# A softmax streamed through one buffer: four loads become two, and two late loads become one

## The chip, the cores and the metric

The kernel runs on one core of a Trainium2 chip. The metric is device time in microseconds (us) of one execution. Every profile is of one further execution, with times in us from the start of its span.

## The reference

```python
x = np.random.randn(16, 1024, 512).astype(np.float32)
x_scaled = x / 2.0
exp_x = np.exp(x_scaled - np.max(x_scaled, axis=-1, keepdims=True))
out = exp_x / np.sum(exp_x, axis=-1, keepdims=True)
```

This is a softmax over 512 elements for each of 16,384 rows, at temperature 2. Input and output have 33.55 MB each, and nothing is read twice, so 67.1 MB have to pass the DMA engines.

## The kernel before, in words

**Tiles.** The 16,384 rows are 128 per partition. In this text "a row" is one such row on all 128 partitions: 512 floats on each, 2 KB a partition, 256 KB in all. `TILES` cuts the 128 rows into ten tiles, numbered 0 to 9: 3, 5, and then eight times 15 rows, each with its place in the buffer. The buffer, `arena`, holds 98 rows. Tiles 0 to 7 fill it; tile 8 comes to rows 0 to 14 and tile 9 to rows 15 to 29, over what tiles 0 to 3 held. A tile of r rows is read from a contiguous block of memory so that partition p gets one contiguous run of r rows; a 15-row tile is 128 runs of 30,720 bytes. The output has the same layout.

**Loads** (`load`, L114). SP (the queue called q1 in the profile) issues the load of tile 0, and ACT (q10) at once the loads of tiles 1 to 7, one DMA each, before it computes anything. GpSimd (POOL, q0) issues the two late loads. It first waits until the exponentials of all rows ahead of row 83 are done (`TURN`, L178: tiles 0 to 6), then, for each late tile, until the stores that free its place have landed: `LATE` says stores 0, 1, 2 for tile 8 and store 3 for tile 9 (L179 to L181). Each load has its semaphore `ld`. TensorE does nothing but pass these on (L196): when load t has landed, it raises `s_go` by the number of chunks in tile t.

**Exponentials** (`exponentials`, L275 in the profile; L206 for the first three rows). ACT takes one unit of `s_go` per chunk of 5 rows, and for each row writes exp(x/2) over the row in place and its sum into `stats`. There is no maximum; the data need none, and a fallback at the end redoes everything if a sum is out of range. It does not run here.

**Division** (L168, L171). DVE takes the reciprocals of the sums of one tile (of 5 rows for the last tile), and multiplies the tile in place.

**Stores** (`store`, L135 to L139). SP issues them in the order of the tiles, each after its multiplication. `SPREAD = 1` makes the store of tile 1 three DMAs: four rows of it as 128 runs of 8,192 bytes, then the fifth row as 126 runs of 2,048 bytes, then the same row's last 2 runs. Before store 2, SP waits until stores 0 and 1 have landed in all their pieces (L214, L215; the profile shows this as a wait of L137 for a DMA). The stores behind it in SP's program wait with it. At the end SP waits for the last landings (L261).

Each transfer of 128 runs is spread over the core's 16 DMA engines, 8 runs on each, and every engine finishes its share with one 4-byte write to the semaphore, here called its marker. In the profile each run and each marker is one packet. A 15-row tile has 128 + 16 = 144 packets.

Of the kernel before, what the change touches and what calls it, by code (L numbers as in the profile page):

```python
# [10 lines left out]
    (3, 0), (5, 3), (15, 8), (15, 23), (15, 38), (15, 53), (15, 68), (15, 83), (15, 0), (15, 15),  # L11
]

LATE = {8: (0, 1, 2), 9: (3,)}
ARENA = 98

HEAD = [3]
# [2 lines left out]
SPREAD = 1  # L20
# [8 lines left out]
def kernel(  # L29
# [5 lines left out]
    nc = tc.nc  # L35
# [6 lines left out]
    xf = x.flatten_outer_dims()  # L42
    of = out.flatten_outer_dims()
    N, D = xf.shape
    P = nc.NUM_PARTITIONS
# [14 lines left out]
    tiles, base = [], 0  # L60
# [2 lines left out]
        tiles.append((base, r, at))  # L63
        base += r

    def dram(ap, t):
        b, r, _ = tiles[t]
        return ap[b * P : (b + r) * P].rearrange("(p r) d -> p r d", r=r)

    def sb(t):  # L70
        _, r, at = tiles[t]
        return arena[:, at : at + r, :]

    straight = sum(HEAD)
# [3 lines left out]
    owner = [max(t for t, (b, _, _) in enumerate(tiles) if b <= s) for s in starts]  # L78
# [9 lines left out]
            pairs.append([k])  # L88
    upto = [1 + max(j for j, ks in enumerate(pairs) if owner[ks[0]] == t) for t in range(len(tiles))]

    ld = [nc.alloc_semaphore(f"ld{t}") for t in range(len(tiles))]
    s_home = {t: nc.alloc_semaphore(f"s_home{t}") for t in LATE}
    s_near = nc.alloc_semaphore("s_near")
    s_end = nc.alloc_semaphore("s_end")
    s_exp = nc.alloc_semaphore("s_exp")
    s_go = nc.alloc_semaphore("s_go")
    s_rec = nc.alloc_semaphore("s_rec")
    s_mul = nc.alloc_semaphore("s_mul")
# [11 lines left out]
    g_rec = nc.alloc_semaphore("g_rec")  # L110
    g_mul = nc.alloc_semaphore("g_mul")

    def load(eng, t):
        eng.dma_start(out=sb(t), in_=dram(xf, t)).then_inc(ld[t], 16)  # L114

    def pieces(t):
        r = tiles[t][1]
        if t == SPREAD:
            return [(0, P, 0, r - 1), (0, 126, r - 1, r), (126, P, r - 1, r)]
        return [(0, P, 0, r)]  # L120

    stored_by = {u: s_home[t] for t, us in LATE.items() for u in us}
    for t, (_, r, at) in enumerate(tiles):
        over = {u for u, (_, ru, au) in enumerate(tiles[:t]) if at < au + ru and au < at + r}
        assert over <= {u for v, us in LATE.items() if v <= t for u in us}

    def landings(ts):
        return 16 * sum(len(pieces(t)) for t in ts)

    near = len(tiles) - 2  # L130
    sem_of = {**stored_by, near: s_near}
    at_end = landings(t for t in range(len(tiles)) if t not in sem_of)

    def store(eng, t):
        eng.wait_ge(s_mul, upto[t])  # L135
        for p, q, lo, hi in pieces(t):
            eng.dma_start(  # L137
                out=dram(of, t)[p:q, lo:hi], in_=sb(t)[p:q, lo:hi]
            ).then_inc(sem_of.get(t, s_end), 16)  # L139

    def take(eng, sem, n):
        eng.wait_ge(sem, n).then_inc(sem, -n)  # L142

    def rounds(eng, body):


        i = eng.alloc_register("general")
        eng.wait_ge(s_near, 16)
        eng.wait_ge(s_flag, 1)
        eng.reg_load(i, flag[0:1, 0:1])  # L150
        with eng.While(lambda: eng.snap(i, min_val=0, max_val=1) < 1):
            body()
            eng.reg_add(i, i, 1)

    def early():
        load(nc.sync, 0)
        load(nc.scalar, 1)

    def loads():
        for t in range(2, min(LATE)):  # L160
            load(nc.scalar, t)

    def program():

        for j, ks in enumerate(pairs):
            b, c = starts[ks[0]], sum(sizes[k] for k in ks)
            a = b % ARENA
            nc.vector.reciprocal(  # L168
                out=recip[:, b : b + c], in_=stats[:, b : b + c]
            )._wait_ge(s_exp, ks[-1] + 1).then_inc(s_rec, 1)  # L170
            nc.vector.tensor_mul(  # L171
                out=arena[:, a : a + c],
                in0=arena[:, a : a + c],
                in1=recip[:, b : b + c].unsqueeze(2).to_broadcast([P, c, D]),
            )._wait_ge(s_rec, j + 1).then_inc(s_mul, 1)

        nc.gpsimd.memset(ones[:, :], 1.0).then_inc(s_ones, 1)  # L177
        nc.gpsimd.wait_ge(s_exp, starts.index(TURN))  # L178
        for t, us in LATE.items():  # L179
            nc.gpsimd.wait_ge(s_home[t], landings(us))  # L180
            load(nc.gpsimd, t)  # L181
        nc.gpsimd.tensor_scalar(  # L182
            out=inside[:, :], in0=stats[:, :], scalar1=LO, scalar2=HI,
            op0=Alu.max, op1=Alu.min,
        )._wait_ge(s_exp, len(sizes)).then_inc(s_cnt, 1)
        nc.vector.scalar_tensor_tensor(  # L186
            out=inside[:, :], in0=inside[:, :], scalar=1.0, in1=stats[:, :],
            op0=Alu.mult, op1=Alu.is_equal, accum_out=count[:, :],
        )._wait_ge(s_cnt, 1).then_inc(s_cnt, 1)
        nc.vector.tensor_scalar(  # L190
            out=flag[:, :], in0=total[:, :], scalar1=float(N), scalar2=None, op0=Alu.is_ge,
        )._wait_ge(s_tot, 1).then_inc(s_flag, 1)


        for t in range(len(tiles)):
            nc.tensor.wait_ge(ld[t], 16).then_inc(s_go, owner.count(t))  # L196
        nc.tensor.wait_ge(s_ones, 1)
        nc.tensor.matmul(  # L198
            total[:, :], lhsT=count[:, :], rhs=ones[:, :], start=True, stop=True
        )._wait_ge(s_cnt, 2).then_inc(s_tot, 1)  # L200

        nc.scalar.preload_act_table(Exp)  # L202
        for k, c in enumerate(HEAD):
            take(nc.scalar, s_go, 1)
            for b in range(starts[k], starts[k] + c):
                ins = nc.scalar.activation(  # L206
                    out=arena[:, b], in_=arena[:, b], func=Exp, scale=0.5,
                    accum_out=stats[:, b : b + 1],
                )
            ins.then_inc(s_exp, 1)  # L210
        exponentials(straight, n_rows)

        for t in range(len(tiles)):
            if t == SPREAD + 1:  # L214
                nc.sync.wait_ge(s_home[min(LATE)], landings(range(t)))  # L215
            store(nc.sync, t)

        x_g = xf.rearrange("(t p r) d -> t p r d", p=P, r=G)  # L220
        o_g = of.rearrange("(t p r) d -> t p r d", p=P, r=G)
        data = arena[:, 0:G]

        def vector():
            for i in range(n_rows // G):
                nc.vector.reduce_max(
                    out=g_max[:, :], in_=data, axis=mybir.AxisListType.X, negate=True
                )._wait_ge(g_go, i + 1).then_inc(g_top, 1)
                nc.vector.reduce_sum(
                    out=g_sum[:, :], in_=data, axis=mybir.AxisListType.X  # L230
                )._wait_ge(g_exp, i + 1).then_inc(g_add, 1)
                nc.vector.reciprocal(
                    out=g_sum[:, :], in_=g_sum[:, :]
                )._wait_ge(g_add, i + 1).then_inc(g_rec, 1)

        def scalar():
            for i in range(n_rows // G):
                nc.scalar.activation(out=data, in_=data, func=Exp, scale=0.5)._wait_ge(
                    g_sub, i + 1
                ).then_inc(g_exp, 1)  # L240

        def gpsimd():
            nc.gpsimd.wait_ge(s_end, at_end)
            for i in range(n_rows // G):
                nc.gpsimd.dma_start(out=data, in_=x_g[i]).then_inc(g_ld, 16)
                nc.gpsimd.wait_ge(g_ld, 16 * (i + 1)).then_inc(g_go, 1)
                nc.gpsimd.tensor_add(
                    out=data, in0=data, in1=g_max[:, :].unsqueeze(2).to_broadcast([P, G, D])
                )._wait_ge(g_top, i + 1).then_inc(g_sub, 1)
                nc.gpsimd.tensor_mul(  # L250
                    out=data, in0=data, in1=g_sum[:, :].unsqueeze(2).to_broadcast([P, G, D])
                )._wait_ge(g_rec, i + 1).then_inc(g_mul, 1)
                nc.gpsimd.wait_ge(g_mul, i + 1)
                nc.gpsimd.dma_start(out=o_g[i], in_=data).then_inc(g_st, 16)
                nc.gpsimd.wait_ge(g_st, 16 * (i + 1))

        rounds(nc.vector, vector)
        rounds(nc.scalar, scalar)
        rounds(nc.gpsimd, gpsimd)
        nc.sync.wait_ge(s_near, 16)  # L260
        nc.sync.wait_ge(s_end, at_end)  # L261
# [26 lines left out]
    first = list(entry.instructions)  # L288
    at = next(k for k, i in enumerate(head) if type(i).__name__ == "InstDrain")
    entry.instructions = head[:at] + first + head[at:]  # L290
    act = []
    entry.instructions = list(entry.instructions) + [i for i in jumps if i not in act]
    nc.switch_body(here, parent=None, valid_engines=[i.engine for i in jumps])
    loads()
    program()


# [28 lines left out]
```

## Time and profile before

| | |
|---|---|
| median of 3 runs | 159.98 us (159.81 to 159.98) |
| profiled execution: time | 159.75 us |
| profiled execution: span | 158.4 us |
| busy: ACT, DVE, POOL, PE | 80.6, 73.2, 2.2, 0.2 us |
| DMA packets, bytes | 3024, 67.11 MB |
| DMA, mean over the span | 424 GB/s |
| load of tile 7: issued, landed | 4.30, 84.4 us |
| late loads: issued | 73.94, 92.71 us |
| stores of tiles 2, 3, 4, 5: issued | 49.08, 49.48, 57.95, 67.23 us |
| stores of tiles 6, 7, 8, 9: issued | 82.14, 102.57, 116.04, 128.84 us |

The DMA rows give, for each queue, its packets, their bytes, and the time that its packets took as a share of the 16 engines' time in the span or in a window of it. "Issued" is the start of the issuing instruction; "landed" is its time to landing added to that.

### The profile page before, as it was taken

Reading aid. Unit: us, or ns where it says so; the run is one execution under the profiler, and the core shown is the slowest. Engines: PE = TensorE matmul, PEld = TensorE weight load, DVE = VectorE, ACT = ScalarE, POOL = GpSimd, SP = SyncE. Lnnn points to the kernel's source line nnn. Section 1 sums busy time; section 2 is a strip of 40 time slices with the busy share of each in tenths; the row PEclk is TensorE's granted clock in tenths of the full one; section 3 lists DMA queues with packets and bytes.
Section 4 is the critical chain, followed back from the end, with each engine's and each line's share of the span. In section 5 each row is a group of like instructions: output and inputs, shape, how many; then the busy total and the mean of one; then the engine's idle time right before and its main releaser. Section 6 shows DMA issues by size and latency. Waiting matters only on the chain. (4 is left out here: it accounts for less than half of the span.)

```text
span 158.4 us, 658 instructions
## 1 busy us (share of the span) xinstructions
PE 0.2 (0%) x2; PEld 0.1 (0%) x2; DVE 73.2 (46%) x27; ACT 80.6 (51%) x257; POOL 2.2 (1%) x8
## 2 busy tenths in 40 slices
PE   0000000000000000000000000000000000000000
PEld 0000000000000000000000000000000000000000
DVE  0066000992994979903970029808927960000000
ACT  0780399598899980795005971991059700000000
POOL 0000000000000000001000010000000100000000
DMA  7999998999999999999898989898989898989896
GB/s 270 469 411 383 461 439 357 446 470 412 395 502 389 442 427 427 442 411 458 388 481 380 489 380 489 380 489 380 489 372 496 372 489 380 489 380 489 380 481 264
DMA packets 3024, 67.11 MB, mean 424 GB/s; under 512 B 336, under 2 KB 336, under 8 KB 720
## 3 DMA queue, kind: packets, MB, share of 16 engines
q1 hardware_dynamic: 1728, 34.34, 50.7%
q10 hardware_dynamic: 1008, 24.90, 37.0%
q0 software_dynamic: 288, 7.86, 11.5%
HBM read 33.55 MB, written 33.55 MB: 424 GB/s over the span
## 5 line engine op out<-in xcount | busy, mean ns | idle before, releaser
L275 ACT ACTIVATE arena<-arena x125 | 76.7, 615 | 40.2 <-ACTq L142 40.2
L171 DVE TENSOR_TENSOR arena<-arena,recip 128x7680 f32<-128x7680 f32 (+2 forms) x12 | 70.2, 5847 | 0.4
L168 DVE RECIPROCAL recip<-stats 128x15 f32<-128x15 f32 (+2 forms) x12 | 2.7, 224 | 55.5 <-ACT arena L275 47.3
L275 ACT ACTIVATION_READ_ACCUMULATOR arena<-arena x125 | 23.4, 187 | 0.0
L202 ACT ACT_TABLE_LOAD x1 | 1.3, 1283 | 5.0 <-issue 5.0
L114 POOL DMA_DIRECT2D arena<-in_x_dram x2 | 1.3, 631 | 90.3 <-ACT arena L275 72.3
L206 ACT ACTIVATE arena<-arena 128x512 f32<-128x512 f32 x3 | 1.9, 618 | 0.0
L182 POOL TENSOR_SCALAR inside<-stats 128x128 f32<-128x128 f32 x1 | 0.6, 631 | 32.6 <-ACT arena L275 32.6
L206 ACT ACTIVATION_READ_ACCUMULATOR arena<-arena 128x1 f32 x3 | 0.6, 185 | 0.0
L198 PE MATMUL total<-ones,count 128*1 128x1 f32 x2 | 0.2, 164 | 129.1 <-DVE inside L186 129.1
L186 DVE SCALAR_TENSOR_TENSOR inside<-inside,stats 128x128 f32<-128x128 f32 x1 | 0.3, 284 | 0.0
L190 DVE TENSOR_SCALAR flag<-total 1x1 int32<-1x1 f32 x1 | 0.1, 147 | 0.3 <-PE total L198 0.3
L198 PEld LDWEIGHTS total<-ones,count 128*1 128x1 f32 x2 | 0.1, 80 | 129.1 <-DVE inside L186 129.1
L177 POOL MEMSET ones<- 128x1 f32 x1 | 0.1, 99 | 1.1 <-POOLq L37 1.1
L310 POOL MEMSET const-float32-0.0<- 128x1 f32 x1 | 0.1, 105 | 0.2 <-issue 0.2
L310 POOL MEMSET const-bfloat16-1.0<- 128x1 bf16 x1 | 0.1, 108 | 0.0
L310 POOL MEMSET const-uint8-127<- 128x1 uint8 x1 | 0.1, 108 | 0.0
L310 POOL MEMSET const-float32-1.0<- 128x1 f32 x1 | 0.1, 105 | 0.0
L186 DVE DVE_READ_ACCUMULATOR inside<-inside,stats 128x1 f32 x1 | 0.1, 83 | 0.0
## 6 DMA issues: line engine op xcount, KB each, us to landing
out_dram<-arena SPq DMA_DIRECT2D x8, 3840.0 KB, 42.9
arena<-in_x_dram ACTq DMA_DIRECT2D x6, 3840.0 KB, 41.7
arena<-in_x_dram POOLq DMA_DIRECT2D x2, 3840.0 KB, 23.7
arena<-in_x_dram ACTq DMA_DIRECT2D x1, 1280.0 KB, 7.3
out_dram<-arena SPq DMA_DIRECT2D x1, 1024.0 KB
arena<-in_x_dram SPq DMA_DIRECT2D x1, 768.0 KB, 5.9
out_dram<-arena SPq DMA_DIRECT2D x1, 768.0 KB
out_dram<-arena SPq DMA_DIRECT2D x1, 252.0 KB
```

Of the source, the lines that this page charges most:

```text
L114: eng.dma_start(out=sb(t), in_=dram(xf, t)).then_inc(ld[t], 16)
L168: nc.vector.reciprocal(out=recip[:, b : b + c], in_=stats[:, b : b + c])._wait_ge(s_exp, ks[-1] + 1).then_inc(s_rec, 1)
L171: nc.vector.tensor_mul(out=arena[:, a : a + c], in0=arena[:, a : a + c], in1=recip[:, b : b + c].unsqueeze(2).to_broadcast([P, c, D]),)._w ...
L177: nc.gpsimd.memset(ones[:, :], 1.0).then_inc(s_ones, 1)
L182: nc.gpsimd.tensor_scalar(out=inside[:, :], in0=stats[:, :], scalar1=LO, scalar2=HI, op0=Alu.max, op1=Alu.min,)._wait_ge(s_exp, len(sizes) ...
L186: nc.vector.scalar_tensor_tensor(out=inside[:, :], in0=inside[:, :], scalar=1.0, in1=stats[:, :], op0=Alu.mult, op1=Alu.is_equal, accum_ou ...
L190: nc.vector.tensor_scalar(out=flag[:, :], in0=total[:, :], scalar1=float(N), scalar2=None, op0=Alu.is_ge,)._wait_ge(s_tot, 1).then_inc(s_f ...
L198: nc.tensor.matmul(total[:, :], lhsT=count[:, :], rhs=ones[:, :], start=True, stop=True)._wait_ge(s_cnt, 2).then_inc(s_tot, 1)
L202: nc.scalar.preload_act_table(Exp)
L206: ins = nc.scalar.activation(out=arena[:, b], in_=arena[:, b], func=Exp, scale=0.5, accum_out=stats[:, b : b + 1],)
L275: ins = nc.scalar.activation(out=data, in_=data, func=Exp, scale=0.5, accum_out=stats[:, r : n_rows - E + 1 + r][:, bass.ds(now, 1)],)
L310: nc = _bacc.Bacc("TRN2", target_bir_lowering=False, num_devices=1)
```

## The change

The lists `LOADS` and `STORES` say which tiles go together in one DMA. The stores stay one for each tile. Of the loads, tiles 4 and 5 become one, tiles 6 and 7 become one, and the late tiles 8 and 9 become one. A pair of loads reads one block of 30 rows per partition, so its 128 runs are 61,440 bytes long; partition p's rows in memory are then 30 neighbours, of which the first tile of the pair has 15 and the second 15. Stores of these tiles write half of such a block: 128 runs of 30,720 bytes as before, now 61,440 bytes apart. A pair has one semaphore, so the second tile's and the first tile's chunks are let go together. `LATE` becomes `{6: (0, 1, 2, 3)}`: the one late load waits for stores 0 to 3. SP's wait ahead of store 2 still asks for stores 0 and 1.

```diff
-LATE = {8: (0, 1, 2), 9: (3,)}
+LOADS = [(0,), (1,), (2,), (3,), (4, 5), (6, 7), (8, 9)]
+STORES = [(0,), (1,), (2,), (3,), (4,), (5,), (6,), (7,), (8,), (9,)]
+
+LATE = {6: (0, 1, 2, 3)}
...
-    def dram(ap, t):
-        b, r, _ = tiles[t]
-        return ap[b * P : (b + r) * P].rearrange("(p r) d -> p r d", r=r)
...
+    def dram(ap, ts):
+        b, r, _ = span(ts)
+        first, rows, _ = next(blocks[k] for k, us in enumerate(LOADS) if ts[0] in us)
+        assert first <= b and b + r <= first + rows
+        block = ap[first * P : (first + rows) * P].rearrange("(p r) d -> p r d", r=rows)
+        return block[:, b - first : b - first + r]
...
-    def load(eng, t):
-        eng.dma_start(out=sb(t), in_=dram(xf, t)).then_inc(ld[t], 16)
...
+    def load(eng, k):
+        eng.dma_start(out=sb(LOADS[k]), in_=dram(xf, LOADS[k])).then_inc(ld[k], 16)
...
-        for t in range(2, min(LATE)):
-            load(nc.scalar, t)
+        for k in range(2, min(LATE)):
+            load(nc.scalar, k)
...
-        for t, us in LATE.items():
-            nc.gpsimd.wait_ge(s_home[t], landings(us))
-            load(nc.gpsimd, t)
+        for k, js in LATE.items():
+            nc.gpsimd.wait_ge(s_home[k], landings(js))
+            load(nc.gpsimd, k)
...
-        for t in range(len(tiles)):
-            nc.tensor.wait_ge(ld[t], 16).then_inc(s_go, owner.count(t))
+        for k, ts in enumerate(LOADS):
+            nc.tensor.wait_ge(ld[k], 16).then_inc(
+                s_go, sum(owner.count(t) for t in ts)
+            )
...
-        for t in range(len(tiles)):
-            if t == SPREAD + 1:
-                nc.sync.wait_ge(s_home[min(LATE)], landings(range(t)))
-            store(nc.sync, t)
+        for j in range(len(STORES)):
+            if j == SPREAD + 1:
+                nc.sync.wait_ge(s_home[min(LATE)], landings(range(j)))
+            store(nc.sync, j)
```

## The prediction

> **What bounds the kernel now.** I read the page's slices and queues first, then SP's waits, then the DMA queues in narrow windows. Slices, and the queues' shares of 16 engines:
>
> ```profile
> DMA  7999998999999999999898989898989898989896
> ...
> q1 hardware_dynamic: 1728, 34.34, 50.7%
> q10 hardware_dynamic: 1008, 24.90, 37.0%
> q0 software_dynamic: 288, 7.86, 11.5%
> ```
>
> The shares add to 99.2% of the span. ACT (80.6 us) and DVE (73.2 us) have half of it idle. So the end is set by bytes through the DMA engines, and computing matters only where it leaves the engines without work. A change can win only packet overhead; it loses every microsecond in which no queue holds a packet. The waits of SP, which issues all stores:
>
> ```profile
> SPq L261 <- DMA out_dram<-arena: 29.2, 1, 29.2
> ...
> SPq L137 <- DMA out_dram<-arena: 13.0, 1, 13.0
> ```
>
> The 29.2 us are the last stores draining. The 13.0 us are the hold ahead of store 2, until stores 0 and 1 have landed; the timeline has the issue that ends it:
>
> ```profile
> 49.08 0.84 SPq L137 DMA_DIRECT2D out_dram<-arena  x2
> ```
>
> How two queues share an engine decides the rest. Windows 29.5 to 33.5 us (8,192-byte store runs against 30,720-byte load runs), 41 to 46 (2,048 against 30,720) and 54 to 62 (equal sizes); packets, MB, share of 16 engines:
>
> ```profile
> q10 hardware_dynamic: 41, 1.26, 72.9%
> q1 hardware_dynamic: 42, 0.34, 20.3%
> ```
> ```profile
> q10 hardware_dynamic: 64, 1.97, 91.0%
> q1 hardware_dynamic: 58, 0.12, 6.1%
> ```
> ```profile
> q10 hardware_dynamic: 63, 1.94, 56.0%
> q1 hardware_dynamic: 49, 1.51, 43.6%
> ```
>
> Whatever the sizes, packets come about one for one (in the second window two of the 16 engines have no store runs, so 14 of 16 is the expected ratio). A store of small runs is therefore slowed to the pace of the load's runs. Shares times 16 engines times the window, over packets, give the cost of one: 0.91 x 80 / 64 = 1.138 us for 30,720 bytes, 0.203 x 64 / 42 = 0.309 for 8,192, 0.061 x 80 / 58 = 0.084 for 2,048. The first two give 0.0368 us per 1,000 bytes and 0.008 us fixed, so 61,440 bytes should take 2.268 us.
>
> **Part 1, fewer packets.** Each of the three pairs takes 8 data packets from every engine: 24 x 0.008 = 0.19 us gained. The markers saved have no size. Three issues less on ACT and POOL are worth nothing: ACT's are done by 5 us and ACT is idle later, POOL is idle.
>
> **Part 2, loads 4 to 7 against the held stores.** Nothing differs until tile 3's load ends, whose markers lie on most engines between 27.5 and 28.1 us; I count from 27.65, 20.85 ahead of 48.5. Count packets from there to the hold's last one. In the window 27.5 to 48.4 us, q1 had 12.6% of 20.9 us, 2.63 us per engine; 16 load runs (tiles 4 and 5) are 16 x 1.138 = 18.2; together 20.8, which ends at 48.5. The window 48.2 to 48.6 us confirms the place:
>
> ```profile
> q10 hardware_dynamic: 26, 0.40, 233.0%
> q1 hardware_dynamic: 4, 0.00, 2.9%
> ```
>
> q1's four packets are the last two 2 KB runs and their markers, at the moment at which tile 5's load ends: the held stores run out as the 18th load packet passes (2 x 8 runs, 2 markers). Behind it, ACT's queue still held tiles 6 and 7, which covered SP's 0.5 us from marker to issue (48.5 to 49.08) and the start of store 2.
>
> Afterwards 18 load packets are pair (4,5) and pair (6,7), which is everything that ACT's queue has. 16 x 2.268 = 36.3, and 2.6 of stores: 27.65 + 38.9 = 66.6 us. At 66.6 the last load and the hold end on the same packet, and no queue holds anything. The late load is not there: POOL waits for store 3, which is behind the hold. So all 16 engines idle from 66.6 until store 2's first packet: 0.53 us marker to issue, and the start of a DMA. On idle queues only the opening shows that; windows 0 to 1 us and 1 to 1.3 us after SP's first issue at 0.00:
>
> ```profile
> DMA packets 0, 0.00 MB, mean 0 GB/s; under 512 B 0, under 2 KB 0, under 8 KB 0
> ```
> ```profile
> q1 hardware_dynamic: 14, 0.09, 153.1%
> ```
>
> Hence 1.0 us, and a gap of 1.55. Bounds: at the short side 1.25, since an engine that is 0.3 us late at 66.6 (three of 16 markers of tile 5's load come after 48.6) idles less; at the long side the opening's second transfer, issued at 0.12, starts at about 2.5, so 0.53 + 2.4 = 2.9. Store 2 today starts 3.9 us after its issue, but 48 load packets, three per engine, pass in between (window 49.1 to 52.9), 3.4 us, which leaves 0.5. I take 1.55, as SP's issue is the first on idle queues, like the opening's. The Trainium skill ("DMA: Bandwidth & Descriptors", Latency and other measured facts) gives about 0.6 us to the first byte; by it the gap would be 1.1 and the forecast below 0.45 us lower.
>
> **Part 3, computing and the late load.** Pair (4,5) lands about 48.2 (27.65 + 18.1 + 1.95 of stores + 0.5), not 39.8 and 49.1; tile 4's store is ready at 66.5 instead of 57.9, covered by stores 2 and 3, which run 68.15 to 86.35 (16 x 1.138). Pair (6,7) lands at 67.1; tile 6's exponentials (15 x 0.61 = 9.2) end at 76.5, which satisfies L178; tile 6's and 7's products end at 85 and 94.5 (8.4 each). Stores 4 to 7 so keep q1 full. The late load issues at 86.9, when store 3 has landed; its predecessor needed 4.2 us from issue (73.94) to first packet (none of q0 until 78.1), so 91.1. Its 8 runs alternate with stores: 8 x (2.268 + 1.138) = 27.2, to 118.3. Exponentials from 119.2, and store 8 issued 17.8 later as before (98.24 to 116.04): 137.0, first packet 138.0. Stores 4 to 7 last until 86.35 + 32 x 1.138 + 18.1 = 140.9. Cover left: 2.9 us. Store 9 is ready at 146.2, needed at 150.0. Each microsecond beyond that cover would go to the end.
>
> **Sum.** From 68.15: 64 store runs x 1.138 + 8 x 2.268 = 91.0, last data at 159.1, against 48.5 + 96 x 1.138 = 157.75 now by the same count. That is +1.35 (1.55 - 0.19, rounded). On the profiled execution's 159.75: 161.1 us. The median stands 0.23 above that execution, so 161.3.
>
> **Rivals.**
> *The hold ends while a load run is still queued* (not slower). If the store queue got ahead by one load packet, its 2.27 us would cover the 1.55, and only part 1 is left: 159.98 - 0.19 = 159.8. It decides from a lead of one packet in 18. For: the tie is exact, so little tips it. Against: packets alternated one for one in three windows of different sizes. The Trainium skill (same page, Queues, rings and completion order) says that an engine drains a whole packet of 9 to 17 descriptors from one queue before it turns to the next; by that, a store's nine entries would pass in one turn, the hold would end early, and the time would be this rival's; 41 against 42 and 64 against 58 speak against it.
> *61,440-byte runs are cut in two.* Then loads 4 to 7 keep their pace: no gap at 66.6, but (6,7) lands near 82, L178 passes at 91.9, the late load starts at 96.1 and takes 32 turns of 1.138 to 132.5; store 8 starts at 152.1, while the stores ahead end at 140.3: a gap of 11.8, 171.6 us. If only POOL's is cut: 91.1 + 36.4 = 127.5, store 8 starts at 147, stores end at 141.0: 161.3 + 6 = 167.3. The trace has no run over 30,720 bytes, and none seen cut.
> *Late cover gone*: the late load starts 3 to 5 us later than 91.1, and store 8 is up to 2 us late: 161.3 to 163.3.
>
> **How the numbers follow.** Forecast as summed 0.71 (161.0 to 162.7), hold covered 0.14 (159.8), runs cut 0.09 (167 to 172), late cover gone 0.06. The range 159.5 to 163.0 leaves out about 0.11. A measurement here tells 0.2%, 0.32 us, from no change. Overhead alone cannot pass that: faster 0.06 (half of the covered case, if overheads are larger than I sized), same 0.08, slower 0.86.
>
> **What would show it.** 2592 packets (three pairs save 3 x 144), q10 720, q0 144. Around 67 us one or two slices of low DMA share with nothing in any queue; SP's hold 31 us instead of 13.0, ended near 67.1; one POOL wait for a DMA, to about 87. Wrong would be: 3024 minus only markers (runs cut), tile 6 before 60 or after 75 us, no gap at 67, or a gap ahead of store 8 near 141.

## The result: 2.55 us slower, and the profile after

Five runs of the changed kernel have a median of 162.46 us (162.36 to 162.91) against 159.91 for the kernel before in the same comparison; the ratio is 1.0166, interval 1.0152 to 1.018. The profiled execution took 162.48 us with a span of 161.2, that is 2.7 us more than before in the time and 2.8 in the span. Forecast were 161.3 us and a range of 159.5 to 163.0: the sign and the range held, but the forecast rise of 1.35 us is about half of the measured one.

The page's slices, packets and queues of the kernel after:

```profile
DMA  7999999797996999389999979989998989999996
...
DMA packets 2592, 67.11 MB, mean 416 GB/s; under 512 B 288, under 2 KB 288, under 8 KB 672
...
q1 hardware_dynamic: 1728, 34.34, 50.4%
q10 hardware_dynamic: 720, 24.90, 36.2%
q0 software_dynamic: 144, 7.86, 11.7%
```

The packets are as forecast, so a 61,440-byte run is one packet. The 17th slice (64.5 to 68.5 us) shows a hole that the kernel before has not. (The shares of the slices, and of the windows below, count a packet where it starts. With runs of 2.27 us a lower digit, such as the 6 of the 13th slice, need not be idle time.) SP's hold ahead of store 2 and POOL's wait, in the tables of waits:

```profile
SPq L155 <- DMA out_dram<-arena: 31.1, 1, 31.1
```
```profile
POOL arena L128 <- DMA out_dram<-arena: 85.7, 1, 85.7
```

The hold has grown from 13.0 to 31.1 us. The timeline has SP's issue at its end (67.10 forecast as "near 67.1") and POOL's (forecast 86.9):

```profile
67.10 1.80 SPq L155 DMA_DIRECT2D out_dram<-arena  x3
```
```profile
87.40 0.72 POOL L128 DMA_DIRECT2D arena<-in_x_dram  x1 [85.73 <-DMA out_dram<-arena]
```

Two stretches lose time, 66 to 68 us and 92 to 97 us. In these windows of busy time the last two columns are the DMA share and GB/s; from 97 us on the rate is full again:

```profile
66.00:68.00 2.00, 0.00 (x0) 0.00 (x0) 1.25 (x2) 2.00 (x7) 0.00 (x0) 1.00 0.26 110
...
92.00:97.00 5.00, 0.00 (x0) 0.00 (x0) 2.58 (x1) 0.00 (x0) 0.00 (x0) 1.00 1.15 375
97.00:130.00 33.00, 0.00 (x0) 0.00 (x0) 0.00 (x0) 8.31 (x27) 0.00 (x0) 1.00 1.00 433
```

The kernel before, from 66 to 68 us and where its first late load starts, 77 to 82 us:

```profile
66.00:68.00 2.00, 0.00 (x0) 0.00 (x0) 1.20 (x1) 2.00 (x8) 0.00 (x0) 1.00 1.00 430
77.00:82.00 5.00, 0.00 (x0) 0.00 (x0) 5.00 (x1) 0.00 (x0) 0.00 (x0) 1.00 1.01 436
```

*The first gap.* At 66 to 68 us the engines are idle: the DMA window from 66.8 to 67.9 us holds no packet at all,

```profile
DMA packets 0, 0.00 MB, mean 0 GB/s; under 512 B 0, under 2 KB 0, under 8 KB 0
```

the loads' 16 markers all come before it, from 66 us on, and all 16 first runs of store 2 start between 67.9 and 68.2. From the forecast end of the loads, 66.6, that is about 1.4 us of idle.

*The second loss.* At 92 to 97 us the share is full and the rate is not: packets take longer. It is where POOL's late load starts beside stores alone. Per queue, in the DMA windows 92 to 97 and 97 to 102 us (packets, MB, share):

```profile
q0 software_dynamic: 16, 0.98, 58.3%
q1 hardware_dynamic: 29, 0.89, 56.5%
```
```profile
q0 software_dynamic: 32, 1.97, 91.0%
q1 hardware_dynamic: 19, 0.58, 27.0%
```

Share times 80 over packets gives 2.92 us for a long run and 1.56 for a store run in the first five microseconds, 2.28 and 1.14 in the next five. The 1.56 is a mean of two kinds. All 16 engines start a store run within the 0.15 us from 92.0 to 92.15, and these took 1.90 us each (12.674 x 16 engines x 0.15 us over 16 runs), although the load's first run starts only at 93.6:

```profile
q1 hardware_dynamic: 16, 0.49, 1267.4%
```

The other 13 store runs of the window took 1.14 (45.2 - 16 x 1.90 = 14.8, over 13). So each engine has one stretched store run, the one ahead of the load's first run, and then one stretched long run. The excess, (29 x 0.42 + 16 x 0.65) / 16, is 1.4 us per engine; as shares of 115% say that packets overlap a little, it is an upper bound. The balance gives the same size: from store 2's first packets at 68.0 the forecast's count of the remaining work is 91.0, which ends at 159.0; the last markers come after 160.2.

So 1.4 idle, about 1.3 stretched, less some 0.2 for packets saved: 2.5 us.

### The profile page after: what moved, and what is told of

Read it like the earlier page. It is cut to its first block, busy times and chain, and to the rows that moved or that the text cites. A ratio compares the mean times of both kernels' runs of the same rounds, so it can differ in the third digit from the quotient of the medians.

```text
span 161.2 us, 652 instructions
## 1 busy us (share of the span) xinstructions
PE 0.2 (0%) x2; PEld 0.1 (0%) x2; DVE 72.9 (45%) x27; ACT 80.2 (50%) x257; POOL 3.7 (2%) x7
## 2 busy tenths in 40 slices
DMA packets 2592, 67.11 MB, mean 416 GB/s; under 512 B 288, under 2 KB 288, under 8 KB 672
## 5 line engine op out<-in xcount | busy, mean ns | idle before, releaser
L200 POOL TENSOR_SCALAR inside<-stats 128x128 f32<-128x128 f32 x1 | 2.6, 2646 | 52.1 <-ACT arena L295 52.1
L128 POOL DMA_DIRECT2D arena<-in_x_dram x1 | 0.7, 722 | 85.7 <-DMA out_dram<-arena 85.7
```

Source lines behind the costliest of these rows:

```text
L128: eng.dma_start(out=sb(LOADS[k]), in_=dram(xf, LOADS[k])).then_inc(ld[k], 16)
L200: nc.gpsimd.tensor_scalar(out=inside[:, :], in0=stats[:, :], scalar1=LO, scalar2=HI, op0=Alu.max, op1=Alu.min,)._wait_ge(s_exp, len(sizes) ...
```

## The experiments

The first theory was of two separate losses: the gap, as forecast, and a loss at the late load's start, for which there were three candidates: any load that joins stores alone ("join"), its first run of 61,440 bytes ("size"), or POOL's queue ("software queue").

### The first gap, and the start of the late load

**The changed kernel without the hold.**

```diff
         for j in range(len(STORES)):
-            if j == SPREAD + 1:
-                nc.sync.wait_ge(s_home[min(LATE)], landings(range(j)))
             store(nc.sync, j)
```

> The changed kernel without SP's wait ahead of store 2 (the wait only paces; POOL's own wait for stores 0 to 3 stays). Theory of two gaps: the changed kernel loses about 1.4 us at 66.4 to 68.0 us, where the hold ends together with the last early load, and about 1.3 us at 92 to 97 us, where the late load starts beside stores alone. Without the hold, store 2 is queued behind store 1 and the first gap goes: about 161.1 us (162.46 - 1.4), and the windows around 67 us are full. Rival (the whole loss comes with the long runs or the late load, and the gap at 67 us is made up elsewhere): stays at 162.4.

Measured: 160.84 us median, but spread from 160.35 to 162.63 over four runs; ratio to before 1.0101, interval 1.004 to 1.0161. In the profiled execution (160.35 us) the window from 64 to 68 us is full:

```profile
64.00:68.00 4.00, 0.00 (x0) 0.00 (x0) 4.00 (x1) 4.00 (x15) 0.00 (x0) 1.00 1.10 447
```

The gap is the hold's, as the theory said. The medians differ by 1.6 us, which the spread does not tell from the expected 1.4; but the profiled execution, the fastest of the four, got back 2.1. In it the late load's first runs, at 92 to 97 us, take 2.35 us each, so most of the second loss went too, which neither theory had said. In its place there is a small new gap: pair (6,7) lands only at 78.4 us, POOL issues the late load 1.3 us later than in the changed kernel (88.73), store 8 is issued as late as there (139.38) though the stores ahead of it end sooner, and the window from 137 to 142 us has a DMA share of 0.92, about 0.4 us. What made the other three executions slower is in no trace.

**The late load as two of 15 rows.**

```diff
-LOADS = [(0,), (1,), (2,), (3,), (4, 5), (6, 7), (8, 9)]
+LOADS = [(0,), (1,), (2,), (3,), (4, 5), (6, 7), (8,), (9,)]
...
-LATE = {6: (0, 1, 2, 3)}
+LATE = {6: (0, 1, 2, 3), 7: ()}
...
-            nc.gpsimd.wait_ge(s_home[k], landings(js))
+            if js:
+                nc.gpsimd.wait_ge(s_home[k], landings(js))
```

> The changed kernel with the late load cut back into two loads of 15 rows (runs of 30,720 bytes) that are issued one after the other, both behind stores 0 to 3, by the same queue at the same time. Theory join (the loss at 92 to 97 us belongs to a load that starts while only stores run, whatever its runs): the loss there stays about 1.3 us and the time 162.5. Theory size (it belongs to the first run of 61,440 bytes): the loss falls to about half, 161.8. If tile 8 now lands earlier, that changes nothing, since store 8 was not late.

Measured: 162.57 us (ratio 1.0169, 1.0152 to 1.0186). The store runs at 92 to 97 us still take 0.637 x 80 / 32 = 1.59 us in the mean:

```profile
q1 hardware_dynamic: 32, 0.98, 63.7%
```

The size theory falls.

**The late load issued by ACT.**

```diff
-        nc.gpsimd.wait_ge(s_exp, starts.index(TURN))
-        for k, js in LATE.items():
-            nc.gpsimd.wait_ge(s_home[k], landings(js))
-            load(nc.gpsimd, k)
...
-        exponentials(straight, n_rows)
+        exponentials(straight, ARENA)
+        for k, js in LATE.items():
+            nc.scalar.wait_ge(s_home[k], landings(js))
+            load(nc.scalar, k)
+        exponentials(ARENA, n_rows)
```

> The changed kernel with the late load of 30 rows issued by ACT between the exponentials of tile 7 and tile 8, behind the same four stores, and not by POOL. ACT is idle there, so the issue comes at about the same 87 us. Theory software queue (the loss at 92 to 97 us comes from how POOL's queue starts): it goes, about 161.2 us. Theories join and size: it stays, within 0.3 us of 162.5; the load may start some us earlier.

Measured: 163.06 us (1.0199, 1.0182 to 1.0216), 0.3 us outside of what was expected of any theory. Issued at 86.92 us, the load has its first run at 91.9; at 90 to 95 us:

```profile
q10 hardware_dynamic: 16, 0.98, 66.3%
q1 hardware_dynamic: 15, 0.46, 35.5%
```

That is 3.3 us for a long run and 1.9 for a store run, even more than by POOL. The software queue falls too.

**The kernel before with its late loads as late.**

```diff
-TURN = 83
+TURN = 98
```

> The kernel before, all loads single, with TURN 98 instead of 83: POOL issues the first late load about 94 us, when ACT's loads have long landed, so that it too starts beside stores alone, with runs of 30,720 bytes. No gap at 67 us. Theory join and theory software queue: about 1.3 us lost at its start, 161.2 us. Theory size: nothing lost, 159.9 us. If store 8 becomes late (tile 8 should land about 119, its store be ready about 137, the stores ahead last until about 138), up to 1 us more.

Measured: 159.99 us (1.0011, 1.0001 to 1.002). POOL issues both late loads at 92.16 us, beside stores alone, and nothing is lost; 96 to 101 us:

```profile
q1 hardware_dynamic: 39, 1.20, 55.5%
q0 software_dynamic: 32, 0.98, 45.5%
```

1.138 us each. So "join" falls as well: a load may join stores alone at no cost. None of the three candidates is the cause by itself.

### A second theory: the loss follows an idle restart

What the losers have in common is that all engines had been idle and restarted on one store. One trace of that is left when the late load comes: in the changed kernel all 16 engines start a store run within the 0.15 us from 92.0 to 92.15, while with TURN 98 no window of that length, in the 2.4 us ahead of the load's first run, holds more than 10. These 10 (96.40 to 96.55 us) took 4.763 x 0.15 x 16 / 10 = 1.14 us each, in place of 1.90:

```profile
q1 hardware_dynamic: 10, 0.31, 476.3%
```

I called this "lockstep" and made it the next theory.

**Tiles 6 and 7 loaded singly.**

```diff
-LOADS = [(0,), (1,), (2,), (3,), (4, 5), (6, 7), (8, 9)]
+LOADS = [(0,), (1,), (2,), (3,), (4, 5), (6,), (7,), (8, 9)]
...
-LATE = {6: (0, 1, 2, 3)}
+LATE = {7: (0, 1, 2, 3)}
```

> The changed kernel with tiles 6 and 7 loaded singly again; pair (4,5), the late load of 30 rows, the hold and POOL's wait stay. Gap theory: when the hold ends, about 58 us, tile 7's load is still queued, so the 1.4 us gap goes. Theory lockstep (new: the 1.3 us at the late load's start are lost only where all 16 engines restarted together after a gap and so turn to the load within 0.15 us of each other): that loss goes too, about 159.9 us, the time of the kernel before. Rival (the second loss is independent of the gap): 161.1.

Measured: 160.26 us (1.003, 1.0014 to 1.0047). The hold is 22.3 us, ending while tile 7's load is queued. At 90 to 95 us, where the late load starts:

```profile
q1 hardware_dynamic: 33, 1.01, 47.2%
q0 software_dynamic: 16, 0.98, 45.7%
```

1.144 and 2.285 us: without the gap the second loss is gone as well, with the same late load of 61,440-byte runs. Of the 0.35 us above the expected time, some 0.26 lie where store 2 joins tile 7's load: 33 load runs at 60 to 64 us take 0.688 x 64 / 33 = 1.33 us, where the kernel before has 1.21 at the same event (51 to 55 us). The two windows:

```profile
q10 hardware_dynamic: 33, 1.01, 68.8%
```
```profile
q10 hardware_dynamic: 33, 1.01, 62.3%
```

So a queue that joins can cost something without idle engines before it, though here much less.

**The late half of the change alone.**

```diff
-LOADS = [(0,), (1,), (2,), (3,), (4, 5), (6, 7), (8, 9)]
+LOADS = [(0,), (1,), (2,), (3,), (4,), (5,), (6,), (7,), (8, 9)]
...
-LATE = {6: (0, 1, 2, 3)}
+LATE = {8: (0, 1, 2, 3)}
```

> Half of the change alone: tiles 4 to 7 loaded singly, and one late load of 30 rows behind stores 0 to 3. No gap at the hold's end. Theory lockstep: 159.9 us, the late load costs nothing although it starts beside stores alone. Rival (a run of 61,440 bytes that joins stores alone loses 1.3 us): 161.2.

Measured: 160.02 us (1.0017, 0.9998 to 1.0037), not told from no change. From 90.9 to 95.9 us, where the late load starts, its long runs take 2.30 us and the store runs 1.14. The joint late load costs next to nothing by itself.

**The early half alone.**

```diff
-LOADS = [(0,), (1,), (2,), (3,), (4, 5), (6, 7), (8, 9)]
+LOADS = [(0,), (1,), (2,), (3,), (4, 5), (6, 7), (8,), (9,)]
...
-LATE = {6: (0, 1, 2, 3)}
+LATE = {6: (0, 1, 2), 7: (3,)}
```

> The other half alone: pairs (4,5) and (6,7), and two late loads behind stores 0 to 2 and store 3 as before. The gap stays (1.4 us at 66.5 to 68). The first late load starts about 78 us after its issue condition, store 2, beside engines that restarted together: lockstep says another 1.3 us there, 162.5 us in all; the rival that the second loss belongs to the joint late load says 161.2.

(The load of tile 8 was issued at 78.27 us; "78 us after its condition" was misworded.) Measured: 162.38 us (1.0157, 1.0138 to 1.0175). The early pairs alone have the whole cost, both losses; at 82 to 87 us a store run takes 0.601 x 80 / 32 = 1.50 us in the mean:

```profile
q1 hardware_dynamic: 32, 0.98, 60.1%
q0 software_dynamic: 16, 0.49, 27.1%
```

**A pause put into the kernel before**, on top of TURN 98 (`s_home[9]` is raised by store 3 alone):

```diff
         for t in range(len(tiles)):
...
+            if t == 4:
+                nc.sync.wait_ge(s_home[9], 16)
             store(nc.sync, t)
```

> The kernel before with TURN 98 (which alone took 159.99 us, with no loss where the late load joins) and one more wait of SP: store 4 is issued only when store 3 has landed. ACT's loads have ended by then, so all engines idle about 1.4 us near 86 us and restart together. Lockstep: 1.4 for the pause and about 1.3 more where the late load starts, about 97 us: 162.7 us. Rival (what made the second loss is the changed kernel's memory layout, or its runs): 161.4.

Measured: 162.60 us (1.0171, 1.0154 to 1.0188). The windows show the pause (84 to 88 us), and the loss at the late load's start (97 to 102 us), with the old layout and 30,720-byte runs:

```profile
84.00:88.00 4.00, 0.00 (x0) 0.00 (x0) 0.00 (x0) 4.00 (x14) 0.00 (x0) 1.00 0.66 276
97.00:102.00 5.00, 0.00 (x0) 0.00 (x0) 3.33 (x1) 0.00 (x0) 0.00 (x0) 1.00 1.03 375
```

The window from 85.4 to 86.5 us holds no packet. The store runs at 97 to 102 us take 1.54 us in the mean; the 16 that start in the 0.15 us from 96.97, ahead of the load's first run, took 13.389 x 0.15 = 2.01 each. The two windows:

```profile
q1 hardware_dynamic: 29, 0.89, 55.9%
```
```profile
q1 hardware_dynamic: 16, 0.49, 1338.9%
```

The same pair of loads joins the same stores as with TURN 98 alone; one idle restart 10 us earlier makes the difference. Together with the two runs (no hold, and tiles 6 and 7 loaded singly) in which taking the idle stretch away took most or all of the loss away, this shows that the second loss follows the idle restart. What the restart leaves behind that makes it is not shown.

### Lockstep itself: four runs that did not settle it

To separate "all at the same moment" from "something that the restart leaves in each engine", store 4 was cut so that small runs pull the engines apart, once with the pause and once without, both on top of TURN 98. The fifteenth row becomes 14 small DMAs: one of 64 partitions and 13 of 8, 4 and 2 (the expectations say 13 in all).

```diff
+        if t == 4:
+            cuts = [0, 64] + [64 + 8 * k for k in range(1, 6)]
+            cuts += [104 + 4 * k for k in range(1, 5)] + [120 + 2 * k for k in range(1, 5)]
+            return [(0, P, 0, r - 1)] + [(p, q, r - 1, r) for p, q in zip(cuts, cuts[1:])]
```

> Control for the next one: the kernel before with TURN 98, and store 4 cut into 14 rows as 128 runs and the 15th row as 13 small DMAs of 64, 8, 4 and 2 partitions, so that some engines get up to 13 more runs of 2,048 bytes (0.084 us each) than others and the engines pull apart by 0, 0.4, 0.8 and 1.1 us. No pause. The engine with most work ends about 0.8 us above the mean: 160.0 to 160.9 us, by both theories, and no loss where the late load starts.

> The same with SP's extra wait (store 4 only when store 3 has landed): the engines idle about 1.4 us and restart together, but the uneven small runs pull them apart before the late load starts near 97 us. Theory lockstep (the second loss needs all 16 engines to turn to the load at the same moment): the pause costs its 1.4 us over the control and the load's start little, 0 to 0.6. Rival (the second loss comes from what an idle restart leaves in each engine by itself, for instance the overlap of successive runs seen after it): 1.4 + 1.2 = 2.6 us over the control.

Measured: 161.81 us (1.0136, 1.0116 to 1.0155) and 165.85 us (1.0377, 1.0359 to 1.0395). The control came out 0.9 us above its range, partly because store 8 was late (a DMA share of 0.86 from 148 to 151 us). Nor was the late load's start free, as had been expected: the store runs at 96 to 101 us take 0.616 x 80 / 38 = 1.30 us:

```profile
q1 hardware_dynamic: 38, 1.17, 61.6%
```

With the pause, the 14 small DMAs, issued one by one, left the engines without work about 95 us, and the late load started among them:

```profile
94.00:96.00 2.00, 0.00 (x0) 0.00 (x0) 2.00 (x1) 0.00 (x0) 0.00 (x0) 1.00 0.56 127
```

So it made a second idle stretch, and says nothing about the first. The next pair put the small runs into the middle of store 4 (the edit against the one above):

```diff
-            return [(0, P, 0, r - 1)] + [(p, q, r - 1, r) for p, q in zip(cuts, cuts[1:])]
+            small = [(p, q, 8, 9) for p, q in zip(cuts, cuts[1:])]
+            return [(0, P, 0, 8)] + small + [(0, P, 9, r)]
```

> Second control: TURN 98, and store 4 as 8 rows, then its 9th row as the 13 small DMAs, then 6 rows. The engines are pulled apart by up to 1.1 us, and all small runs are over by 92 us, before the late load starts near 97 us. No pause. 160.3 to 161.8 us (uneven work 0.8, and a late store 8 as in the first control), with under 0.4 us lost where the late load starts.

> The same with the pause ahead of store 4. All engines restart together near 86.5 us, are pulled apart by the small runs about 91 us, and meet the late load near 97 us with runs of 30,720 bytes in both queues. Lockstep: the control plus 1.4 us for the pause, and under 0.6 us lost at 96 to 100 us, mostly by the eight engines that the small runs leave together. Rival (an idle restart leaves each engine in a state that costs 1.2 us at the load's start, wherever the others are): the control plus 2.6, with about 1.2 us lost there.

Measured: 161.94 us (1.0117, 1.01 to 1.0134) and 165.26 us (1.0315, 1.0273 to 1.0358). With the pause, the small runs again went through faster than SP issued them, and the late load started by 94 us, ahead of the last six rows of store 4, so this run does not decide either. The control has no pause, and yet its store runs at 96 to 101 us, where the late load joins, take 0.541 x 80 / 33 = 1.31 us:

```profile
q1 hardware_dynamic: 33, 1.01, 54.1%
```

That is an excess of (33 x 0.17) / 16, 0.35 us an engine. So some loss is possible without an idle restart, here with engines that are not in step (at most 7 of 16 start a store run in any 0.15 us of the 2.4 ahead of the load). Why the runs stretch stays open.

## Why the prediction was right or wrong

- **The bound** (DMA engines 99.2% busy, so only overhead can be won and only idle or stretched engines lose): right. No variant was faster than the kernel before, and TURN 98, which kept its time, has full engines in the windows shown.
- **One packet for one, whatever its size**: right, also at 61,440 bytes. In the window from 49 to 64 us,

```profile
q10 hardware_dynamic: 96, 5.90, 90.7%
q1 hardware_dynamic: 84, 0.17, 2.9%
```

  84 is 14/16 of 96, and 0.907 x 240 / 96 = 2.268 us, the forecast price. The hold's last runs passed with the last load's, so the store queue got no lead, and the rival that needed one did not come. The Trainium skill ("DMA: Bandwidth & Descriptors", Queues, rings and completion order) says that an engine drains a whole packet of descriptors, 9 to 17 typically, from one queue before it switches. This trace, with 84 against 96, does not agree.
- **The hold and the last load end together at 66.6 us**: right; the issue was forecast at 67.1 and came at 67.10.
- **The gap, 1.55 us**: right, about 1.4. Store 2's first packet came 0.86 us after its issue, where the forecast had the opening's 1.0. The Trainium skill ("DMA: Bandwidth & Descriptors", Latency and other measured facts) gives about 0.6 us to the first byte; this trace has more.
- **Cover of store 8, 2.9 us**: it held, though tighter. Store 8 was issued at 139.48, 2.5 us later than forecast, since the late load's first packet came 6.2 us after its issue (87.40 to 93.6) and not 4.2, and then was stretched.
- **The step that failed is the sum**: "64 store runs x 1.138 + 8 x 2.268 = 91.0, last data at 159.1". It gave every packet after 68.15 the price of a steady stretch, and so put the start of the late load at nothing. That start cost about 1.3 us. In the kernel before the late load's start had indeed cost nothing (1.137 us a run of q0 from 77 to 82 us). But the same trace has two other places where a queue joins and runs get longer: from 12 to 17 us, where store 0 joins the loads, 61 load runs took 0.965 x 80 / 61 = 1.27 us, an excess of about 0.5 us an engine, and from 51 to 55 us 33 of them took 1.21, about 0.14. The prediction read its prices in steady windows only. This is why +1.35 became +2.55 (the gap 0.15 less, this start 1.3 more).
- **The range**: that 162.46 us still lies in it is in part luck. Neither the sum nor a rival has a loss at the late load's start.
- **Rivals**: runs cut in two was refuted by the 2592 packets, hold covered by the window from 66.8 to 67.9 us without a packet. Late cover gone did not happen here, but did so in the kernel without the hold, by 0.4 us.

## What to carry to other kernels

Where two DMA queues share engines packet for packet, the size of a run sets the share: longer load runs slow every small store beside them (58 runs of 2,048 bytes passed in 5 us beside runs of 30,720 bytes, 84 in 15 us beside runs of 61,440), and a wait tuned to end while loads are still queued can then end on an empty queue. Count packets, not bytes, to see which queue runs out first, and count what empty queues can cost twice: the idle itself, and, as here, the next time that a second stream joins. Here three DMAs less could bring 0.2 us at best, and the hole they opened cost over ten times that.

## What the runs showed of the hardware that was not expected

After all engines idled for about 1.4 us, the start of the next load beside the stores, 12 to 26 us later, cost some 1.2 to 1.9 us per engine, with 30,720- and 61,440-byte runs, from POOL's and from ACT's queue, with both layouts (1.2 from 162.60 - 159.99 less the idle; 1.9 with ACT's load, 0.6 above the changed kernel). Without the idle the same load joined at 1.14 us a run. The stretch begins ahead of the load: the store run that each engine starts before the load's first run took 1.90 us in the changed kernel and 2.01 after the pause, in place of 1.14, and the next ones were back at about 1.14. The load's own first runs took 2.92 us in place of 2.27 when they had 61,440 bytes, and 1.16 to 1.35 in place of 1.14 when they had 30,720. The kernel before has something like it, smaller, where its first store joins the loads 13 us after the start from empty queues (1.27 us a run from 12 to 17 us); that this has the same cause is not shown. That all engines start their runs within about 0.15 us of each other (16 in that time after the pause, too, from 96.97) is a correlate, not a shown cause.
